# A softmax-minus-one-hot kernel with all large transfers on one queue, in whole blocks and a fixed order

## The chip, the cores and the metric

The kernel runs on one core of a Trainium2 chip. The metric is the device time of one execution in microseconds; lower is better. Bytes move between the chip's main memory and the core's on-chip buffer over sixteen DMA engines, which serve one queue for each engine that issues transfers: here SP's (SyncE's) and ACT's (ScalarE's).

## What is computed

For each of 8 x 1024 rows of 8192 float32 logits the reference computes the softmax and subtracts 1 at the label's place. It is the gradient of a cross entropy.

```python
logits_max = np.max(logits, axis=-1, keepdims=True)
exp_logits = np.exp(logits - logits_max)
softmax = exp_logits / np.sum(exp_logits, axis=-1, keepdims=True)
...
one_hot[batch_idx, seq_idx, labels] = 1.0
return (softmax - one_hot).astype(np.float32)
```

Every logit is read once and every output written once: 268.4 MB in, 268.4 MB out.

## The kernel before

**Tiling.** The 8192 rows are cut into 32 blocks (B) of 256 rows. A block lies as 128 partitions x 2 rows (G = 2) x 8192, so that a partition's two rows are neighbours in memory: 64 KB in one run. A "row" of the code, `t` from 0 to 63, is one of the two 128 x 8192 halves of a block, 4.2 MB; block b holds rows 2b and 2b + 1. The buffer X (line 48) has 3 slots (SLOTS) of one block, and block b uses slot b % 3. All work is done in place.

**One row.** Each operation goes through the helper `run` (lines 70 to 82), which attaches the waits and the semaphore that the operation raises, so most rows of the profile have line 76. `row_max` (line 141) takes the negated maximum on VectorE (TENSOR_REDUCE). `exponentials` takes exp with that bias and the row's sum on ScalarE (ACTIVATE X<-X,m). `mark` makes on ScalarE, in two operations over 2048 words, a byte mask with a 1 at the label (away, then hot, in PSUM, with two places). `finish` takes the reciprocal of the sum on VectorE and then x * r - mask over the row (SCALAR_TENSOR_TENSOR); the last two rows are finished in two halves of 4096 columns each, so that each half can be stored by itself.

**Transfers.** `load` (line 101) and `store` (line 114) issue transfers in pieces that the letters of LOADS and STORES select for each block: "w" is the whole block in one transfer with 64 KB runs, "r" one transfer for each row with 32 KB runs, "s" two transfers for each row, over the even and the odd partitions. Loads are issued on SP's queue, except the odd halves of "s", which go on ACT's. Blocks 0 to 2 are loaded as "s", 3, 4 and 29 to 31 as "r", the rest as "w". Stores are all "r" and are issued on ACT's queue, where each waits for its row's finish; the four half stores of the last block go two on SP and two on ACT. A load waits until the stores of the block that had its slot have landed, and it is issued for block b + 3 after the work of block b.

**Order.** Each engine runs its instructions in the order in which the program issues them. Every letter of ORDER is "r", which interleaves the rows: maximum of t1, finish of t0, exponentials of t1, store of t0, mark; then the next block's first maximum, finish of t1, exponentials of the next row, store of t1, mark, and the load of block b + 3. Before the loop stand the first three loads and the making of the masks' constants. At the end ACT waits for the stores of the last three blocks.

Of the kernel before, what the change touches and what calls it, by code (L numbers as in the profile page):

```python
# [7 lines left out]
P = 128  # L8
G = 2
SLOTS = 3  # L10

LOADS = "sssrrwwwwwwwwwwwwwwwwwwwwwwwwrrr"
STORES = "rrrrrrrrrrrrrrrrrrrrrrrrrrrrrrrr"
ORDER = "rrrrrrrrrrrrrrrrrrrrrrrrrrrrrrrr"


@with_exitstack
def kernel(
# [6 lines left out]
    nc = tc.nc  # L25
# [11 lines left out]
    T = N // P  # L37
    B = T // G
# [3 lines left out]
    o_b = o_nv.rearrange("(b p j) v -> b p j v", p=P, j=G)  # L42
# [4 lines left out]
    X = const.tile([P, SLOTS, G, V], fp32)  # L47
# [11 lines left out]
    m, s, r = (const.tile([P, T], fp32, name=n) for n in ("m", "s", "r"))  # L59
# [4 lines left out]
    with tc.tile_critical():  # L64
        sem = tc.alloc_semaphore
        got = [[sem(f"got{i}{q}") for q in range(4)] for i in range(SLOTS)]
        put = [[sem(f"put{i}{q}") for q in range(4)] for i in range(SLOTS)]
# [3 lines left out]
        def run(engine, waits, counter, method, **operands):  # L71

            waits = list(dict.fromkeys(waits))
            for w in waits[:-1]:
                engine.wait_ge(*w)  # L75
            instruction = getattr(engine, method)(**operands)  # L76
            for w in waits[-1:]:
                instruction._wait_ge(*w)
            step = 16 if method == "dma_start" else 1
            instruction.then_inc(counter, step)  # L80
            count[counter.name] = count.get(counter.name, 0) + step
            return counter, count[counter.name]

        every, rows = slice(0, P), slice(0, G)
        one = [slice(j, j + 1) for j in range(G)]
        halves = [slice(i, P, 2) for i in range(2)]
        sides = [slice(i * V // 2, (i + 1) * V // 2) for i in range(2)]
        PIECES = {
            "r": [(every, js) for js in one],
            "s": [(ps, js) for js in one for ps in halves],  # L90
            "w": [(every, rows)],
        }

# [4 lines left out]
        loaded, stored, sides_done = {}, {}, {}  # L98
        maxed, summed, marked, finished, freed = {}, {}, {}, {}, {}

        def load(b):
            loaded[b] = []
            before = stored.get(b - SLOTS, [])
            for q, piece in enumerate(PIECES[LOADS[b]]):
                ps, js = piece
                free = [w for other, w in before if meets(piece, other)]
                queue = nc.scalar if LOADS[b] == "s" and ps == halves[1] else nc.sync
                w = run(
                    queue, free, got[b % SLOTS][q], "dma_start",
                    out=X[ps, b % SLOTS, js, :], in_=x_b[b, ps, js, :],  # L110
                )
                loaded[b].append((piece, w))

        def store(t):
            b, j = divmod(t, G)
            stored.setdefault(b, [])
            if t >= T - G:
                for i, cs in enumerate(sides):
                    w = run(
                        nc.sync if t == T - G else nc.scalar, [sides_done[t][i]], put[b % SLOTS][G * j + i],  # L120
                        "dma_start", out=o_b[b, every, one[j], cs], in_=X[every, b % SLOTS, one[j], cs],
                    )
                    stored[b].append(((every, one[j]), w))
                return
            for q, piece in enumerate(PIECES[STORES[b]]):
                ps, js = piece
                if js.stop != j + 1:
                    continue
                w = run(
                    nc.scalar, [finished[t]], put[b % SLOTS][q], "dma_start",  # L130
                    out=o_b[b, ps, js, :], in_=X[ps, b % SLOTS, js, :],
                )
                stored[b].append((piece, w))
# [7 lines left out]
        def row_max(t):  # L141
            b, j = divmod(t, G)
            arrived = {w[0].name: w for piece, w in loaded[b] if meets(piece, (every, one[j]))}
            maxed[t] = run(
                nc.vector, arrived.values(), dve, "tensor_reduce",
                out=m[:, t : t + 1], in_=row(t), axis=mybir.AxisListType.X, op=Alu.max, negate=True,
            )

        def exponentials(t):
            w = run(  # L150
                nc.scalar, [maxed[t]], act, "activation",
                out=row(t), in_=row(t), func=Act.Exp, bias=m[:, t : t + 1], scale=1.0,
                accum_out=s[:, t : t + 1],
            )
            summed[t] = w

        def mark(t):
            if t >= T:
                return
            w = run(  # L160
                nc.scalar, ([made] if t < G else [freed[t - G]]) + ([marked[t - 1]] if t else []), act, "activation",
                out=away[:], in_=count16[:], func=Act.Abs, bias=at(word, t), scale=1.0,
            )
            marked[t] = run(
                nc.scalar, [w], act, "activation",
                out=hot[:, t % G, :], in_=away[:], func=Act.Relu, bias=at(unit, t), scale=at(minus, t),
            )

        def finish(t):
            w = run(nc.vector, [summed[t]], dve, "reciprocal", out=r[:, t : t + 1], in_=s[:, t : t + 1])  # L170
            bytes_ = hot[:, t % G, :].bitcast(u8)
            sides_done[t] = []
            for i, c in enumerate(sides if t >= T - G else [slice(0, V)]):
                last = run(
                    nc.vector, [marked[t], w] if i == 0 else [], dve, "scalar_tensor_tensor",
                    out=row(t)[:, c], in0=row(t)[:, c], scalar=r[:, t : t + 1], in1=bytes_[:, c],
                    op0=Alu.mult, op1=Alu.subtract,
                )
                sides_done[t].append(last)
            finished[t] = freed[t] = last  # L180

        w_raw = run(nc.scalar, [], lab_got, "dma_start", out=lab_raw[:], in_=lab_bp)
        for b in range(SLOTS):
            load(b)
        w = run(nc.gpsimd, [], pool, "memset", ap=ident[:], constant=0.0)
        w_ident = run(
            nc.gpsimd, [w], pool, "affine_select",
            out=ident[:], in_=ident[:], compare_op=Alu.not_equal, fill=1.0,
# [8 lines left out]
        for j in range(G):  # L197
            w = run(
                nc.tensor, [w_ident, w_lab], pe, "transpose",
                out=lab_ps[:, j, :], in_=lab_f[:, j, :], identity=ident[:],  # L200
            )
        w = run(nc.vector, [w], dve, "tensor_copy", out=lab[:], in_=lab_ps)
        w = run(
            nc.vector, [w], dve, "tensor_scalar",
            out=part[:], in0=lab[:], scalar1=2, scalar2=None, op0=Alu.arith_shift_right,
        )
        w_word = run(
            nc.vector, [w], dve, "tensor_scalar",
            out=word[:], in0=part[:], scalar1=-1.0, scalar2=None, op0=Alu.mult,
        )  # L210
        w = run(
            nc.vector, [w_word], dve, "tensor_scalar",
            out=lab[:], in0=lab[:], scalar1=3, scalar2=None, op0=Alu.bitwise_and,
        )
        w = run(
            nc.vector, [w], dve, "tensor_copy", out=minus[:], in_=lab[:]
        )
# [3 lines left out]
            out=unit[:], in0=minus[:], scalar1=0.0, scalar2=powers[0], op0=Alu.is_equal, op1=Alu.mult,  # L221
# [15 lines left out]
        nc.scalar.wait_ge(*w_made)  # L237
        made = made_dve

        row_max(0)  # L240
        exponentials(0)
        mark(0)
        mark(1)
        for b in range(B):
            t0, t1 = b * G, b * G + 1
            nxt = t1 + 1
            if ORDER[b] == "b":
                if t0 not in maxed:
                    row_max(t0)
                    exponentials(t0)  # L250
                row_max(t1)
                exponentials(t1)
                finish(t0)
                store(t0)
                mark(t0 + G)
                finish(t1)
                store(t1)
                mark(t1 + G)
                if b + SLOTS < B:
                    load(b + SLOTS)  # L260
                continue
            if t0 not in maxed:
                row_max(t0)
                exponentials(t0)
            row_max(t1)
            finish(t0)
            exponentials(t1)
            store(t0)
            mark(t0 + G)
            ahead = nxt < T and ORDER[b + 1] == "r"  # L270
            if ahead:
                row_max(nxt)
            finish(t1)
            if ahead:
                exponentials(nxt)
            store(t1)
            mark(t1 + G)
            if b + SLOTS < B:
                load(b + SLOTS)
        for b in range(B - SLOTS, B):  # L280
            for _, w in stored[b]:
                nc.scalar.wait_ge(*w)
# [30 lines left out]
```

## Time and profile before

| what | value |
|---|---|
| time, median of 3 runs | 1248.9 us (1247.81 to 1249.44) |
| span of the profiled execution | 1246.6 us (its time with what lies around the span is not shown) |
| TENSOR_REDUCE, 64 of them | 8682 ns each |
| SCALAR_TENSOR_TENSOR over 8192 columns, 62 of them | 8748 ns each |
| read and written | 268.50 MB and 268.44 MB |
| transfers issued on SP / on ACT | 42 / 71 |

How to read the profile: the page gives for each engine its busy time and share of the span. The DMA rows give packets, bytes and how much of the sixteen DMA engines' time each queue's packets took; q1 is SP's queue and q10 is ACT's. A row of groups has the line, engine, operation, output <- inputs, shapes and count, then busy microseconds and mean nanoseconds of one, then the idle time of the engine just before and what ended most of it. A row of windows gives for a stretch its length, the busy time of each engine (and how many instructions ended there), the granted clock of the matrix engine, the mean busy share of the sixteen DMA engines and the rate in GB/s; bytes are counted by packets, so in a window of a few microseconds the rate depends on where its edges fall between packets. A row of DMA issues gives count, KB of one transfer and the median time from issue to landing.

### The profile page before, as it was taken

Reading aid. Unit: us, or ns where it says so; the run is one execution under the profiler, and the core shown is the slowest. Engines: PE = TensorE matmul, PEld = TensorE weight load, DVE = VectorE, ACT = ScalarE, POOL = GpSimd, SP = SyncE. Lnnn points to the kernel's source line nnn. Section 1 sums busy time; section 2 is a strip of 40 time slices with the busy share of each in tenths; the row PEclk is TensorE's granted clock in tenths of the full one; section 3 lists DMA queues with packets and bytes.
Section 4 is the critical chain, followed back from the end, with each engine's and each line's share of the span. In section 5 each row is a group of like instructions: output and inputs, shape, how many; then the busy total and the mean of one; then the engine's idle time right before and its main releaser. Section 6 shows DMA issues by size and latency. Waiting matters only on the chain.

```text
span 1246.6 us, 809 instructions
## 1 busy us (share of the span) xinstructions
PE 0.4 (0%) x2; PEld 0.3 (0%) x2; DVE 1120.2 (90%) x208; ACT 722.7 (58%) x257; POOL 2.3 (0%) x7
## 2 busy tenths in 40 slices
PE   0000000000000000000000000000000000000000
PEld 0000000000000000000000000000000000000000
DVE  5999998889988889888898888998889988899995
ACT  2866664556555565465655655556556555566662
POOL 0000000000000000000000000000000000000000
DMA  9999999999999999999999999999999999999998
GB/s 406 413 431 434 437 432 444 435 437 421 433 429 437 443 423 433 434 431 435 430 441 435 422 435 435 434 440 426 432 434 431 433 446 434 422 430 435 429 434 383
DMA packets 15413, 536.98 MB, mean 431 GB/s; under 512 B 1808, under 2 KB 1808, under 8 KB 1840
## 3 DMA queue, kind: packets, MB, share of 16 engines
q10 hardware_dynamic: 9744, 276.89, 51.5%
q1 hardware_dynamic: 5664, 260.05, 48.3%
q14 instruction: 5, 0.04, 0.0%
HBM read 268.50 MB, written 268.44 MB: 431 GB/s over the span
## 4 chain that ended last, share of the span: by engine, by line
DMA 59%; DVE 26%; issue 11%; ACT 3%; DVEq 0%; ACTq 0%; SPq 0%
DMA X<-in_logits_dram 33%; DMA out_dram<-X 26%; DVE X L76 15%; DVE m L76 10%; ACT X L76 2%; DVEq L64 0%; DVE r L76 0%; ACT hot L76 0%; ACT away L76 0%; ACTq L76 0%; DVEq L75 0%; ACTq L308 0%; SPq L64 0%
## 5 line engine op out<-in xcount | busy, mean ns | idle before, releaser
L76 ACT ACTIVATE X<-X,m 128x8192 f32<-128x8192 f32 x64 | 455.8, 7122 | 365.2 <-DVE m L76 365.2
L76 DVE TENSOR_REDUCE m<-X 128x1 f32<-128x8192 f32 x64 | 555.6, 8682 | 105.4 <-DMA X<-in_logits_dram 105.4
L76 DVE SCALAR_TENSOR_TENSOR X<-X,r,hot 128x8192 f32<-128x8192 f32 (+1 forms) x66 | 560.1, 8489 | 3.8 <-ACT hot L76 1.6
L76 ACT ACTIVATE away<-count,word 128x2048 bf16<-128x2048 int16 x64 | 128.1, 2001 | 127.0 <-DVE X L76 127.0
L76 ACT ACTIVATE hot<-away,unit,minus 128x2048 int32<-128x2048 bf16 x64 | 131.9, 2061 | 2.1
L76 ACT ACTIVATION_READ_ACCUMULATOR X<-X,m 128x1 f32 x64 | 11.9, 186 | 0.0
L76 DVE RECIPROCAL r<-s 128x1 f32<-128x1 f32 x64 | 9.8, 153 | 0.0
L76 ACT ACT_TABLE_LOAD x1 | 1.3, 1283 | 5.3 <-issue 5.3
L76 DVE CAST lab_f<-lab_raw 32x256 f32<-32x256 int32 x1 | 0.5, 536 | 2.7 <-DMA lab_raw<-in_labels_dram 2.7
L76 POOL IOTA count<- 128x2048 int16 x1 | 1.8, 1823 | 0.0
L76 DVE TENSOR_TENSOR unit<-unit,part 128x64 f32<-128x64 f32 x3 | 0.7, 225 | 0.1
L76 DVE CAST lab<-hot 128x64 int32<-128x64 f32 x1 | 0.2, 224 | 0.5 <-PE hot L76 0.5
L76 DVE TENSOR_SCALAR part<-minus 128x64 f32<-128x64 f32 x3 | 0.6, 194 | 0.1
L76 PE MATMUL hot<-ident,lab_f 32*128 32x32 f32 x2 | 0.4, 298 | 3.3 <-DVE lab_f L76 3.3
L76 PEld LDWEIGHTS hot<-ident,lab_f 32*128 32x128 f32 x2 | 0.3, 192 | 3.3 <-DVE lab_f L76 3.3
L76 DVE CAST minus<-lab 128x64 f32<-128x64 int32 x1 | 0.2, 195 | 0.0
L76 DVE TENSOR_SCALAR word<-part 128x64 f32<-128x64 int32 x1 | 0.2, 195 | 0.0
L76 DVE TENSOR_SCALAR lab<-lab 128x64 int32<-128x64 int32 x1 | 0.2, 195 | 0.0
L76 DVE TENSOR_SCALAR unit<-minus 128x64 f32<-128x64 f32 x1 | 0.2, 195 | 0.0
L76 DVE TENSOR_SCALAR part<-lab 128x64 int32<-128x64 int32 x1 | 0.2, 194 | 0.0
L76 DVE TENSOR_SCALAR minus<-unit 128x64 f32<-128x64 f32 x1 | 0.2, 194 | 0.0
L76 POOL TENSOR_SCALAR_AFFINE_SELECT ident<-ident 32x32 f32<-32x32 f32 x1 | 0.2, 203 | 0.1
(5 smaller groups left out, 0.5 us busy)
## 6 DMA issues: line engine op xcount, KB each, us to landing
out_dram<-X ACTq DMA_DIRECT2D x62, 4096.0 KB, 30.4
X<-in_logits_dram SPq DMA_DIRECT2D x10, 4096.0 KB, 28.1
X<-in_logits_dram SPq DMA_DIRECT2D x6, 2048.0 KB, 32.6
X<-in_logits_dram ACTq DMA_DIRECT2D x6, 2048.0 KB, 37.1
out_dram<-X SPq DMA_DIRECT2D x2, 2048.0 KB, 12.7
out_dram<-X ACTq DMA_DIRECT2D x2, 2048.0 KB, 11.9
X<-in_logits_dram SPq DMA_DIRECT2D x24, 33.4
lab_raw<-in_labels_dram ACTq DMA_DIRECT2D x1, 64.0 KB, 1.8
```

What stands on the lines that cost most here:

```text
L76: instruction = getattr(engine, method)(**operands)
```

## The change

- All transfers except the labels' are issued on SP's queue. ACT issues none but the labels'.
- Blocks 0 to 5 and 31 are loaded by rows, 6 to 30 whole. Blocks 0 to 2 and 28 to 30 are stored by rows, 3 to 27 whole; the last block is stored in four half rows, now all on SP. The form "s" is gone.
- `store` is called once for each block, after the work of the block; a whole store waits for the finish of the block's second row.
- The load after the store of block b is that of block b + 3 for b = 0 to 2. After block 3 none is issued (EARLY), so that from block 4 on it is that of block b + 2. After block 27 two are issued (LATE): 29 and 30, and after 28 that of 31.
- The compute order is by block: maximum and exponentials of t0, maximum and exponentials of t1, finish of t0, mark, finish of t1, mark. No operation of the next block stands between them.

```diff
-LOADS = "sssrrwwwwwwwwwwwwwwwwwwwwwwwwrrr"
-STORES = "rrrrrrrrrrrrrrrrrrrrrrrrrrrrrrrr"
-ORDER = "rrrrrrrrrrrrrrrrrrrrrrrrrrrrrrrr"
+EARLY = 3
+LATE = 27
+
+LOADS = "rrrrrrwwwwwwwwwwwwwwwwwwwwwwwwwr"
+STORES = "rrrwwwwwwwwwwwwwwwwwwwwwwwwwrrrr"
...
-                queue = nc.scalar if LOADS[b] == "s" and ps == halves[1] else nc.sync
                 w = run(
-                    queue, free, got[b % SLOTS][q], "dma_start",
+                    nc.sync, free, got[b % SLOTS][q], "dma_start",
...
-        def store(t):
-            b, j = divmod(t, G)
-            stored.setdefault(b, [])
-            if t >= T - G:
...
-                        nc.sync if t == T - G else nc.scalar, [sides_done[t][i]], put[b % SLOTS][G * j + i],
...
+        def store(b):
+            stored[b] = []
+            if b == B - 1:
+                for t in (T - G, T - 1):
...
+                            nc.sync, [sides_done[t][i]], put[b % SLOTS][G * j + i],
...
             for q, piece in enumerate(PIECES[STORES[b]]):
                 ps, js = piece
-                if js.stop != j + 1:
-                    continue
                 w = run(
-                    nc.scalar, [finished[t]], put[b % SLOTS][q], "dma_start",
+                    nc.sync, [finished[b * G + js.stop - 1]], put[b % SLOTS][q], "dma_start",
...
+        def work(b):
+            t0, t1 = b * G, b * G + 1
+            row_max(t0)
+            exponentials(t0)
+            if b == 0:
+                mark(0)
+                mark(1)
+            row_max(t1)
+            exponentials(t1)
+            finish(t0)
+            mark(t0 + G)
+            finish(t1)
+            mark(t1 + G)
+
+        nxt = SLOTS
         for b in range(B):
...
+            work(b)
+            store(b)
+            if b == EARLY:
                 continue
...
+            for _ in range(2 if b == LATE else 1):
+                if nxt < B:
+                    load(nxt)
+                    nxt += 1
```

More of the change, by code (lines that the diff above doesn't have):

```diff
@@ L85 @@
         one = [slice(j, j + 1) for j in range(G)]
-        halves = [slice(i, P, 2) for i in range(2)]
         sides = [slice(i * V // 2, (i + 1) * V // 2) for i in range(2)]
@@ L89 @@
             "r": [(every, js) for js in one],
-            "s": [(ps, js) for js in one for ps in halves],
             "w": [(every, rows)],
@@ L112, in load @@
                 loaded[b].append((piece, w))
-        def store(t):
-            b, j = divmod(t, G)
-            stored.setdefault(b, [])
-            if t >= T - G:
-                for i, cs in enumerate(sides):
-                    w = run(
-                        nc.sync if t == T - G else nc.scalar, [sides_done[t][i]], put[b % SLOTS][G * j + i],
-                        "dma_start", out=o_b[b, every, one[j], cs], in_=X[every, b % SLOTS, one[j], cs],
-                    )
-                    stored[b].append(((every, one[j]), w))
+        def store(b):
+            stored[b] = []
+            if b == B - 1:
+                for t in (T - G, T - 1):
+                    j = t % G
+                    for i, cs in enumerate(sides):
+                        w = run(
+                            nc.sync, [sides_done[t][i]], put[b % SLOTS][G * j + i],
+                            "dma_start", out=o_b[b, every, one[j], cs], in_=X[every, b % SLOTS, one[j], cs],
+                        )
+                        stored[b].append(((every, one[j]), w))
                 return
@@ L238 @@
         made = made_dve
[L240 to L243, printed above, removed]
-        for b in range(B):
[L245 to L260, printed above, removed]
-                continue
[L262 to L279, printed above, removed]
+        def work(b):
[12 more added lines that the diff above has]
+        nxt = SLOTS
+        for b in range(B):
+            work(b)
+            store(b)
+            if b == EARLY:
+                continue
+            for _ in range(2 if b == LATE else 1):
+                if nxt < B:
+                    load(nxt)
+                    nxt += 1
         for b in range(B - SLOTS, B):
```

## The prediction

> **What bounds the kernel now.** I read the page first: busy time, then the DMA rows, then the queues.
>
> ```profile
> span 1246.6 us, 809 instructions
> ...
> PE 0.4 (0%) x2; PEld 0.3 (0%) x2; DVE 1120.2 (90%) x208; ACT 722.7 (58%) x257; POOL 2.3 (0%) x7
> ...
> DMA packets 15413, 536.98 MB, mean 431 GB/s; under 512 B 1808, under 2 KB 1808, under 8 KB 1840
> ## 3 DMA queue, kind: packets, MB, share of 16 engines
> q10 hardware_dynamic: 9744, 276.89, 51.5%
> q1 hardware_dynamic: 5664, 260.05, 48.3%
> ```
>
> VectorE is busy for 90% of the span, but the two transfer queues (q10 is ACT's, q1 is SP's) together fill 51.5 + 48.3 = 99.8% of the sixteen DMA engines. So the transfers are the bound, and VectorE is 10% short of being one. The windows show where the DMA engines move less than their usual rate; the last column is GB/s, the one before it the DMA share.
>
> ```profile
> core 0: us, PE busy (x) PEld busy (x) DVE busy (x) ACT busy (x) POOL busy (x), PEclk, DMA share, GB/s
> 0.00:5.00 5.00, 0.41 (x2) 0.28 (x2) 1.58 (x7) 0.00 (x0) 2.31 (x7) 1.00 0.65 223
> 29.20:58.20 29.00, 0.00 (x0) 0.00 (x0) 27.40 (x6) 26.63 (x11) 0.00 (x0) 1.00 1.01 434
> 58.20:62.80 4.60, 0.00 (x0) 0.00 (x0) 4.60 (x2) 2.52 (x3) 0.00 (x0) 1.00 1.00 342
> 62.80:72.50 9.70, 0.00 (x0) 0.00 (x0) 9.66 (x3) 5.61 (x3) 0.00 (x0) 1.00 1.00 432
> 200.00:1085.00 885.00, 0.00 (x0) 0.00 (x0) 796.30 (x139) 518.52 (x184) 0.00 (x0) 1.00 1.00 433
> 1235.60:1240.40 4.80, 0.00 (x0) 0.00 (x0) 0.00 (x0) 0.00 (x0) 0.00 (x0) 1.00 1.01 430
> 1240.00:1244.00 4.00, 0.00 (x0) 0.00 (x0) 0.00 (x0) 0.00 (x0) 0.00 (x0) 1.00 0.84 360
> 1244.00:1246.60 2.60, 0.00 (x0) 0.00 (x0) 0.00 (x0) 0.00 (x0) 0.00 (x0) 1.00 0.02 6
> ```
>
> All bytes at the steady 433 GB/s are 536.98 MB / 433 = 1240.1 us. What is lost against that rate: 5 x (1 - 223/433) = 2.4 us at the start, 4.6 x (1 - 342/433) = 1.0 us in 58.2 to 62.8, 4 x (1 - 360/433) = 0.7 us and 2.6 us at the end. The sum is 1246.8, the span 1246.6. So nothing is hidden elsewhere: a faster kernel must move the bytes at a better rate or cut the 6.7 us of edges.
>
> **The change, part by part.**
>
> *Fewer, longer packets.* Of the 15413 packets 1808 are the 4-byte notices (16 for each of 113 DMAs). Afterwards 7 blocks load and 6 store as rows (256 packets of 32 KB each), 25 load and 25 store whole (128 packets of 64 KB), and the last block leaves in 512 packets of 16 KB: 1792 + 1536 + 3200 + 3200 + 512 = 10240, where before has 13568 of this data. DMAs fall from 113 to 81, notices by 512. That is 3840 packets fewer. Their price comes from the two queue rows: q10 holds 9744 packets and 276.89 MB in 51.5% of 16 x 1246.6 us, q1 5664 and 260.05 MB in 48.3%. Two equations, "packets x a + MB x c = time", give a = 3.8 ns a packet; the shares are rounded to 0.1%, so a lies between -1.8 and 9.4 ns. The rates of the windows give a second reading: 16 KB runs at 430 and 32 KB runs at 432 GB/s make 5.6 ns. I take 4.7 ns: 3840 x 4.7 / 16 = **1.1 us gained**, bounds -0.4 to 2.3.
>
> *Loads and stores in turn, not mixed.* Today each engine has packets of both queues at hand for most of the span; afterwards one queue holds 8.4 MB of loads, then 8.4 MB of stores. Load-only (434) and store-only (432) stretches ran as fast as the mix (433): I take **0**, with 1 GB/s of 433 either way, 2.9 us, as a bound. Dearer could only be the turn from a load to a store, the second rival below.
>
> *The store's wait on SP.* The store of a block now waits on SP for VectorE's last operation, and behind it in program order stands the load two blocks ahead; behind that load stands VectorE's work on that block. In the steady part the queue reads: load b, store b-1, load b+1, store b. From the end of load b to the place of store b lie 16.78 MB / 433 = 38.75 us of transfers. In that time VectorE must do block b.
>
> ```profile
> L76 DVE TENSOR_REDUCE m<-X 128x1 f32<-128x8192 f32 x64 | 555.6, 8682 | 105.4 <-DMA X<-in_logits_dram 105.4
> L76 DVE SCALAR_TENSOR_TENSOR X<-X,r,hot 128x8192 f32<-128x8192 f32 x62 | 542.4, 8748 | 3.7 <-ACT hot L76 1.6
> L76 ACT ACTIVATE X<-X,m 128x8192 f32<-128x8192 f32 x64 | 455.8, 7122 | 365.2 <-DVE m L76 365.2
> ...
> L76 ACT ACTIVATION_READ_ACCUMULATOR X<-X,m 128x1 f32 x64 | 11.9, 186 | 0.0
> L76 DVE RECIPROCAL r<-s 128x1 f32<-128x1 f32 x64 | 9.8, 153 | 0.0
> ```
>
> Two maxima, two reciprocals, two final operations: 2 x (8.68 + 0.15 + 8.75) = 35.2 us. The new order (both maxima, then both finishes) adds no wait: the first exponentials end at 8.7 + 7.1 + 0.2 = 16.0, before the second maximum ends at 17.4; the second end at 17.4 + 7.3 = 24.7, before the first finish ends at 26.3. So 38.75 - 35.2 = **3.6 us** are left for two latencies: the notice that load b has landed, and the way from SP's issue of the store to its first byte. Before shows neither alone; three rows bound them.
>
> ```profile
> out_dram<-X SPq DMA_DIRECT2D x2, 2048.0 KB, 12.7
> ...
> lab_raw<-in_labels_dram ACTq DMA_DIRECT2D x1, 64.0 KB, 1.8
> ```
>
> The labels' transfer had idle engines: 1.8 us from issue to landing, both latencies and 0.15 us of moving 64 KB. So 1.65 us together. The last stores on SP's queue took 12.7 us for 2.1 MB, which alone are 4.85 us and beside ACT's queue, taking turns, 9.7: both latencies are 3.0 us, or 7.8 if nothing is put down to the other queue. I take 1.8, near the first row, since in one queue nothing stands between. The store then comes 1.8 us early, and the wait costs **0**. Load b+2 behind it waits for store b-1, which landed a load earlier: 0 as well.
>
> *The ends.* Six row loads lie alone on SP's queue, so the first row lands sooner than now.
>
> ```profile
> 15.75 8.69 DVE L76 TENSOR_REDUCE m<-X 128x1 f32<-128x8192 f32 x1 [8.91 <-DMA X<-in_logits_dram]
> ```
>
> It can start near 11 us rather than 15.75, but the queue is then full of loads until 58 us, and VectorE needs the first two rows done only by then (about 51 us with ACT's marks): 0. At the end load 31 stands before stores 29 to 31, 3 x 19.4 us of transfers, while VectorE has at most two blocks of 35.2 us left, of which one is done when the load has landed: 0. The uneven end of the engines (0.7 us) may shrink with one queue: I take 0.3, bounds 0 and 0.7. ACT loses 70 issues and VectorE nothing; neither sets the end.
>
> *Sum.* 1246.6 - 1.1 - 0.3 = 1245.2 us of span. Of the profiled execution only the span is shown; the median of the runs, 1248.9, stands 2.3 us above it, which I take for what lies around a span. With these, **1247.5 us**, 0.11% less. With the bounds: 2.3 + 0.7 us and a little of the 2.9 us of the rate make 1244.6 at the low end, -0.4 and some of the 2.9 make 1249.5 at the high.
>
> **The rivals.**
>
> *1. The same mechanism, more of it.* Packets at the upper bound, an even end, or phases at 434: 1245 to 1246.4, faster by over 0.2%. For it: nothing stands against it but the sizes; the edges that could go are small.
>
> *2. Each turn from load to store in one queue costs (slower).* In 58.2 to 62.8 us ACT's queue ran from its last loads into its first stores, and SP's had just run dry. The engines were busy (share 1.00) and moved 342 GB/s: 1.0 us lost at a turn within one queue. Before has one such turn, as ACT's queue only stores and SP's only loads afterwards. The changed queue has 29: a store behind a load for blocks 0 to 3, 5 to 29 (4, 30 and 31 follow a store). 28 more at 0.97 us are 27 us: 1274.7. It decides from the first turn; nothing covers it, since the DMA engines are the bound. Against it: the mix at 433 GB/s turns at nearly every packet, and the price may be a first filling, or SP's queue running dry.
>
> *3. The store comes late.* If the two latencies exceed 3.6 us, the queue runs dry before the store. The load behind it is put off too, but block b+1 had landed already, so its store gains that time: every second of 25 stores is late, by x - 3.6. At x = 5.4 (between 3.0 and 7.8) 12 x 1.8 = 22 us: 1269. For it: VectorE is the nearest resource to the bound. Against it: two of the three readings stay under 3.6.
>
> The Trainium skill (Perfetto Trace Analysis, DMA Optimizations) advises one engine for inputs and another for outputs, to allow a more dynamic spread. That is what this change gives up, and by that rule the result would be rival 3; here the trace bears it out only in that the two queues never left the engines idle between 200 and 1085 us.
>
> **How the numbers follow.** A measurement of this kernel tells about 0.2% (2.5 us) from no change. No stall: 0.60, of it 0.34 within 0.2% (the forecast) and 0.26 beyond it (rival 1). Rival 2: 0.25. Rival 3: 0.10. Something else, slower: 0.05. So faster 0.26, same 0.34, slower 0.40. The no-stall cases have 1244.6 to 1249.5 as their own range; 0.60 is too little, so the range reaches to the full price of rival 2, 1275, which takes in most of rival 3.
>
> **What the changed profile would show.** Right: one queue with near 99.7% of the sixteen engines, about 11570 packets, 433 to 434 GB/s in the middle, VectorE idle some 3.5 us in each block and always for a load, and SP waiting for VectorE. Rival 2: DMA share still 1.00, but under 428 GB/s. Rival 3: a DMA share under 0.98 with VectorE's idle time unchanged in kind. A span over 1250 us proves the forecast wrong.

## The result and the profile after

The changed kernel takes **1262.7 us** (1261.05 to 1264.52, 4 runs) against 1248.56 for the kernel before in the same sitting. The ratio is 1.0115, with a 95% interval of 1.0100 to 1.0129: 14 us slower. The forecast was 1247.5 and no change; the time lies inside the range, above the cases without a stall (up to 1249.5) and below the prices of rival 3 (1269) and rival 2 (1274.7). One run below, the whole stores on ACT's queue, was profiled in an execution of 1323.9 us where its other three took 1273.3 to 1277.8, so its trace is read for orders of magnitude only.

First the page of the changed kernel: busy time, packets, the queue, and the whole transfers with their median time from issue to landing.

```profile
span 1260.6 us, 747 instructions
...
PE 0.4 (0%) x2; PEld 0.3 (0%) x2; DVE 1120.2 (89%) x208; ACT 722.7 (57%) x257; POOL 2.3 (0%) x7
...
DMA packets 11574, 536.99 MB, mean 426 GB/s; under 512 B 1296, under 2 KB 1296, under 8 KB 1328
...
q1 hardware_dynamic: 11520, 536.88, 99.5%
...
out_dram<-X SPq DMA_DIRECT2D x25, 23.7
X<-in_logits_dram SPq DMA_DIRECT2D x25, 43.1
```

The change does what it says: one queue, 11574 packets (11570 were counted ahead). VectorE has the same work. The DMA engines are marked busy for 99.5%, and yet they move 426 instead of 431 GB/s. The windows of the changed kernel show where; the last two columns are the DMA share and GB/s.

```profile
29.20:58.20 29.00, 0.00 (x0) 0.00 (x0) 24.97 (x6) 23.30 (x12) 0.00 (x0) 1.00 1.01 434
58.20:62.80 4.60, 0.00 (x0) 0.00 (x0) 4.60 (x2) 0.60 (x1) 0.00 (x0) 1.00 0.94 342
200.00:400.00 200.00, 0.00 (x0) 0.00 (x0) 172.97 (x31) 112.78 (x40) 0.00 (x0) 1.00 1.01 434
400.00:600.00 200.00, 0.00 (x0) 0.00 (x0) 178.26 (x32) 113.05 (x41) 0.00 (x0) 1.00 0.99 425
600.00:800.00 200.00, 0.00 (x0) 0.00 (x0) 177.96 (x31) 116.14 (x41) 0.00 (x0) 1.00 1.01 430
800.00:1000.00 200.00, 0.00 (x0) 0.00 (x0) 177.38 (x31) 115.57 (x41) 0.00 (x0) 1.00 1.00 425
200.00:1085.00 885.00, 0.00 (x0) 0.00 (x0) 782.80 (x136) 507.71 (x179) 0.00 (x0) 1.00 1.00 428
1250.00:1260.60 10.60, 0.00 (x0) 0.00 (x0) 0.00 (x0) 0.00 (x0) 0.00 (x0) 1.00 0.59 250
```

The middle lost 885 x (1 - 428/433) = 10.2 us, and the loss begins late: the first 200 us of it run at 434. The last window is compared with the same length at the end of the kernel before:

```profile
1236.00:1246.60 10.60, 0.00 (x0) 0.00 (x0) 0.00 (x0) 0.00 (x0) 0.00 (x0) 1.00 0.69 297
```

There it ran at 297 GB/s, here at 250: 10.6 x (297 - 250)/433 = 1.2 us more. Another 1.5 us went between 1085 and 1250 us, at 428 GB/s where the kernel before had 432 from 1085 to 1236. The three make 12.9 of the 14.0 us between the spans. The first turn from loads to stores costs what it did before, 342 GB/s in the same window.

Why the middle begins well is in the timeline, first at 228, then at 587 us. A row has start, length, engine and operation; in brackets the idle time before.

```profile
228.08 0.33 SPq L77 DMA_DIRECT2D out_dram<-X  x1
228.45 0.43 SPq L77 DMA_DIRECT2D X<-in_logits_dram  x1
238.16 17.28 DVE L77 TENSOR_REDUCE m<-X 128x1 f32<-128x8192 f32 x2 [10.11 <-DMA X<-in_logits_dram]
...
552.27 17.28 DVE L77 TENSOR_REDUCE m<-X 128x1 f32<-128x8192 f32 x2 [5.15 <-DMA X<-in_logits_dram]
...
578.51 8.75 DVE L77 SCALAR_TENSOR_TENSOR X<-X,r,hot 128x8192 f32<-128x8192 f32 x1
587.29 0.33 SPq L77 DMA_DIRECT2D out_dram<-X  x1
587.66 0.43 SPq L77 DMA_DIRECT2D X<-in_logits_dram  x1
591.00 17.28 DVE L77 TENSOR_REDUCE m<-X 128x1 f32<-128x8192 f32 x2 [3.74 <-DMA X<-in_logits_dram]
```

VectorE starts on a block when the last of the sixteen DMA engines has given notice. From 552.27 to 587.29 it needs 35.0 us, as forecast. At 228 us the store is issued ten microseconds before the load ahead of it has landed (238.16). At 587 it is issued 3.7 us before (591.00). That still looks early. But the trace's notices of that load came from 587.87 (first engine) to 590.98 (last): the engines are 3.1 us apart. For the first ones the store was issued 0.6 us before their notice. The packet records show it: on fourteen engines the last packet of the load ended from 587.57 us on, and their first packet of the store started at 588.12, 0.8 us after the issue. They had run dry. The other two engines were one packet behind and ran on without a gap.

The same notices, read for the slowest engine, give each transfer's time as the step from one landing to the next. The 25 whole stores took 19.37 us on average, the 25 whole loads 19.94. Where a store was issued over 1.6 us ahead of the first notice of the load before it, the load behind that store took 19.60 us (mean of 9); where it was issued later, 20.10 (mean of 14); a load with nothing in its way takes 19.3. So the price of a late store shows at the load behind it: 25 x (19.94 - 19.33) = 15 us. The two groups overlap (19.3 to 20.3 and 19.4 to 20.8); these times follow the slowest engine alone.

The packet records of all sixteen engines give a clearer picture. A 64 KB packet mostly takes 2.42 us; around the end of the store that landed at 610 us some took up to 3.5. What the packets around the end of a whole store took beyond 2.42 us, per engine, was 0.88 us on average where the store had been issued under 1 us ahead of that first notice (3 stores), 0.65 at 1 to 1.5 us (9), 0.22 at 1.5 to 2 (6) and 0.06 at over 2 (5). Between 200 and 1085 us such longer packets make 11.4 us per engine, against 3.1 with the half maximum, the first experiment below; the time without any packet differs by only 1.7 us between the two. So for the most part the engines did not stand idle for a late store: they were slow at the turn behind it.

### The profile page after: what moved, and what is told of

It reads as the page before. It is cut to its first block, busy times and chain, and to the rows that moved or that the text cites. A ratio compares the mean times of both kernels' runs of the same rounds, so it can differ in the third digit from the quotient of the medians.

```text
span 1260.6 us, 747 instructions
## 1 busy us (share of the span) xinstructions
PE 0.4 (0%) x2; PEld 0.3 (0%) x2; DVE 1120.2 (89%) x208; ACT 722.7 (57%) x257; POOL 2.3 (0%) x7
## 2 busy tenths in 40 slices
DMA packets 11574, 536.99 MB, mean 426 GB/s; under 512 B 1296, under 2 KB 1296, under 8 KB 1328
## 3 DMA queue, kind: packets, MB, share of 16 engines
q1 hardware_dynamic: 11520, 536.88, 99.5%
## 4 chain that ended last, share of the span: by engine, by line
DVE 50%; DMA 43%; issue 4%; ACT 2%; SPq 0%
DMA X<-in_logits_dram 43%; DVE X L77 25%; DVE m L77 25%; ACT X L77 1%; DVE r L77 1%; ACT hot L77 0%; SPq L77 0%; ACT away L77 0%; SPq L289 0%; SPq L65 0%
## 6 DMA issues: line engine op xcount, KB each, us to landing
X<-in_logits_dram SPq DMA_DIRECT2D x14, 4096.0 KB, 19.4
out_dram<-X SPq DMA_DIRECT2D x25, 23.7
```

## The experiments

Theory A: the store comes late. Theory B: each turn between loads and stores within one queue costs. All are compared with the kernel before, which took 1248.2 to 1248.6 us in each sitting. Differences are to the changed kernel's 1262.7, which was not measured again in the later sittings. The half maximum, the stores by rows, the rows in turn and the whole stores on ACT's queue ran on one chip, the other experiments on another.

### A shorter chain on VectorE

```diff
-                out=m[:, t : t + 1], in_=row(t), axis=mybir.AxisListType.X, op=Alu.max, negate=True,
+                out=m[:, t : t + 1], in_=row(t)[:, : V // 2], axis=mybir.AxisListType.X, op=Alu.max, negate=True,
```

> The changed kernel, but each row's maximum is taken over its first 4096 columns only (the bias of the exponentials; the rest of the row is left out of the maximum). Every transfer, its size, queue and order stay; VectorE's work for a block falls by 2 x 4.3 = 8.7 us, so each whole store is issued some 8.7 us earlier. Theory A (the store comes late: load, 35 us of VectorE and the issue fill the 38.6 us that the queue gives them): the 14 us go, 1246 to 1249 us. Theory B (each turn from load to store or back within one queue costs some 0.5 us whenever the store is issued): stays at 1262.

Measured: 1250.8 us, ratio 1.0019 (1.0010 to 1.0028). 12 of the 14 us go with no transfer changed, so theory A holds and B, which has the same turns, falls. The windows of this run, the middle and the last 10.6 us:

```profile
200.00:1085.00 885.00, 0.00 (x0) 0.00 (x0) 584.16 (x133) 493.80 (x176) 0.00 (x0) 1.00 1.00 433
1240.70:1251.30 10.60, 0.00 (x0) 0.00 (x0) 0.00 (x0) 0.00 (x0) 0.00 (x0) 1.00 0.43 182
```

The middle is back at 433. The end is worse than ever, 182 GB/s: 10.6 x (297 - 182)/433 = 2.8 us more than before, since some engines finish long after others: the notices of the last store lie 6.5 us apart.

### Stores by rows, and rows in turn

```diff
-STORES = "rrrwwwwwwwwwwwwwwwwwwwwwwwwwrrrr"
+STORES = "rrrrrrrrrrrrrrrrrrrrrrrrrrrrrrrr"
```

> The changed kernel with all stores by rows (32 KB runs), still on SP in the same order: the first row's store is issued some 8.8 us before the second's, which is wanted 9.7 us later. Nothing is left out. Theory A: the late store is gone, and 3200 packets more cost about 1 us: 1247 to 1250 us. Theory B: as many turns as before, 1262 to 1264.

Measured: 1253.5 us, ratio 1.0037 (1.0024 to 1.0049). 9 us go; 3.5 more than the upper end of theory A's expectation stay. The load behind the stores was issued no earlier than in the changed kernel: from 300 us on 16.5 to 20.4 us ahead of the first notice of the store it follows, there 20.6 to 21.6. So what counts is when the store was issued, not when the load behind it was. The next kernel also loads by rows and, between block 4 and 26, alternates them:

```diff
+            if EARLY < b < LATE:
+                for j in range(G):
+                    store(b, j)
+                    load(nxt, j)
+                nxt += 1
+                continue
```

> The changed kernel with all transfers by rows, and from block 4 to 26 the one queue holds store of row 0, load of row 0, store of row 1, load of row 1: twice as many turns, and each store is wanted later than it is issued by over 8 us. Nothing is left out. Theory A: 1247 to 1250 us (some 1 to 2 us of it for the shorter packets). Theory B: the price of the turns doubles, near 1276.

Measured: 1251.7 us, ratio 1.0025 (1.0016 to 1.0035). Twice as many turns and 11 us faster: a turn whose store was issued in time costs nothing that can be seen. The middle and the end of both, rows by stores first:

```profile
200.00:1085.00 885.00, 0.00 (x0) 0.00 (x0) 788.42 (x138) 511.63 (x181) 0.00 (x0) 1.00 1.00 432
1242.10:1252.70 10.60, 0.00 (x0) 0.00 (x0) 0.00 (x0) 0.00 (x0) 0.00 (x0) 1.00 0.56 238
```

```profile
200.00:1085.00 885.00, 0.00 (x0) 0.00 (x0) 798.97 (x139) 517.40 (x184) 0.00 (x0) 1.00 1.00 432
1240.20:1250.80 10.60, 0.00 (x0) 0.00 (x0) 0.00 (x0) 0.00 (x0) 0.00 (x0) 1.00 0.48 204
```

Again the middle is mended and the end is not.

### Whole stores on ACT's queue

```diff
-                    nc.sync, [finished[b * G + js.stop - 1]], put[b % SLOTS][q], "dma_start",
+                    nc.scalar, [finished[b * G + js.stop - 1]], put[b % SLOTS][q], "dma_start",
```

> The changed kernel with the whole stores and the row stores (all but the last block's) issued on ACT's queue instead of SP's; sizes, lead and compute order stay. Theory A: a late store no longer leaves the DMA engines dry, since the next load does not stand behind it: 1246 to 1250 us. Theory B: no turns within one queue, so 1246 to 1250 as well. If it stays near 1262, neither the queue nor its order is the cause, but the whole stores or the compute order.

Measured: 1276.9 us, ratio 1.0218 (1.0201 to 1.0236): both theories missed, it is 14 us slower still. The whole transfers in its trace (span 1322.1 us), from issue to landing:

```profile
out_dram<-X ACTq DMA_DIRECT2D x25, 44.0
X<-in_logits_dram SPq DMA_DIRECT2D x25, 41.3
```

In this trace each whole store, beside a load, takes 44.0 us, where the one queue needs 23.7. A load two blocks ahead waits for that landing to get its slot. That this wait is what costs the 14 us is argued, not shown; the next run bears it out only in part, as it makes the stores smaller.

### Row stores on ACT's queue

The edit to row stores and the edit to ACT's queue, together.

> The changed kernel with all stores by rows and on ACT's queue (the last block's four half rows stay on SP): loads, their lead of two and the order of work by block stay. If whole stores beside loads on two queues are what made the run with ACT's stores 15 us slower still (each 8.4 MB transfer then takes 44 us, and the load behind waits for its landing), rows give it back: 1249 to 1254 us. If the order of work by block is what costs, it stays above 1265.

Measured: 1249.2 us, ratio 1.0010 (1.0000 to 1.0019). Against the row stores on SP (1253.5) the kernel differs in the queue alone: two queues are some 4 us better here, measured on two chips. The order of work by block, with the other changes to the loads, leaves 1 us against before. Middle and end of this run:

```profile
200.00:1085.00 885.00, 0.00 (x0) 0.00 (x0) 796.12 (x138) 517.94 (x184) 0.00 (x0) 1.00 1.00 433
1237.00:1247.60 10.60, 0.00 (x0) 0.00 (x0) 0.00 (x0) 0.00 (x0) 0.00 (x0) 1.00 0.66 281
```

### How much earlier is early enough

The maximum over 7/8, 15/16 and 3/4 of the row (`row(t)[:, : 7 * V // 8]` and so on), and one maximum more:

```diff
+            run(
+                nc.vector, arrived.values(), dve, "tensor_reduce",
+                out=r[:, t : t + 1], in_=row(t)[:, : V // 8], axis=mybir.AxisListType.X, op=Alu.max, negate=True,
+            )
```

> The changed kernel with each row's maximum over 7/8 of its columns (the last eighth is left out of the maximum): VectorE's chain for a block is 2.2 us shorter, all else stays. Theory A (the store comes late by little: 0.8 to 1.1 us from issue to first byte where 1.8 cost nothing in the trace of the changed kernel): most of the loss goes, 1250 to 1253 us. Theory C (VectorE's load as such, in proportion): a quarter of what the half maximum took away, 1259 to 1260.

> The same with the maximum over 15/16 of the columns (the last sixteenth is left out): the chain is 1.1 us shorter. Theory A: about half of the loss or more goes, 1252 to 1258 us. Theory C: an eighth, 1261.

> The changed kernel with one more maximum over an eighth of each row, whose result goes where the reciprocal is written later: the chain is 2 x 1.1 = 2.2 us longer, the result the same. VectorE's work on a block becomes 37.4 us, still under the 38.6 us of transfers. Theory A: the round of a store, the load behind it and VectorE's work on that load holds two blocks' transfers and one chain, so each two blocks take 2.2 us more: 12 x 2.2 = 26 us, 1285 to 1292. Theory B (turns): the time stays, 1262 to 1264.

> The changed kernel with the maximum over 3/4 of each row (the last quarter is left out of it): the chain is 4.4 us shorter, between the 7/8 (1258.2) and the half (1250.8). Theory A in the form that the two shorter steps leave (the DMA engines drift apart until the first of them run dry again, so the price fades with the slack and does not stop at once): 1253 to 1256 us.

| chain against the changed kernel | time, us | middle, GB/s | first to last notice at 800 to 900 us | last 10.6 us, GB/s |
|---|---|---|---|---|
| + 2.2 us | 1271.0 | 424 | 0.5 us | 346 |
| as changed | 1262.7 | 428 | 2.7 | 250 |
| - 1.1 us | 1259.5 | 430 | 3.5 | 252 |
| - 2.2 us | 1258.2 | 430 | 4.5 | 235 |
| - 4.4 us | 1255.5 | 431 | 5.3 | 221 |
| - 8.7 us | 1250.8 | 433 | 6.4 | 182 |

Theory A as I first put it missed three of these: 2.2 us were not enough to end the loss (1258.2, not 1250 to 1253), 1.1 us gave 3.2 rather than half of 14 or more, and the longer chain cost 8.3 us and not 26. Theory C, in proportion, would have 1259 to 1260, and 1261 for 1.1 us. That is 1 to 2 us too slow both times, but within the 95% intervals (about 1.9 us either way), so these steps do not exclude it; the longer chain, some 5 us above proportion, and the next experiment, in which VectorE has all of its work and the loss is gone, do. The fourth, made from what the others showed, came within its bounds (1255.5 in 1253 to 1256). The fourth column tells why there is no edge: with more slack the DMA engines drift further apart, until the stores come less than 2 us ahead of the leading ones again. That this drift uses the slack up is read from the table; it was not tried by itself.

Most of the longer chain's price stands in one place. First windows of that run:

```profile
200.00:400.00 200.00, 0.00 (x0) 0.00 (x0) 189.19 (x41) 112.78 (x40) 0.00 (x0) 1.00 0.99 419
400.00:600.00 200.00, 0.00 (x0) 0.00 (x0) 186.48 (x41) 114.78 (x41) 0.00 (x0) 1.00 0.99 425
```

The first 200 us run at 419 (the changed kernel: 434), 200 x (1 - 419/434) = 6.9 us, where all engines ran dry before the store of block 4; afterwards it runs at 425 as the changed kernel does. My 26 us counted two blocks' transfers in a round; a round from landing to landing holds one store and one load, 38.7 us, the chain of 37.2 and about 1.2 of latencies: 77.1, still within the 77.3 that the queue needs for two blocks.

### Whole stores, issued early, with nothing left out

```diff
-LOADS = "rrrrrrwwwwwwwwwwwwwwwwwwwwwwwwwr"
+LOADS = "rrrrrrrrrrrrrrrrrrrrrrrrrrrrrrrr"
```

> The changed kernel with all loads by rows and the stores as they are, whole from block 3 to 27. VectorE can take the first row's maximum while the second row is still arriving, so a block's store is issued some 8.7 us earlier, with nothing left out. Theory A (late whole stores): 1250 to 1253 us, as with the half maximum, 3200 packets more included. If whole stores on one queue cost for another reason than their time of issue (their 64 KB runs, say), it stays near 1262.

Measured: 1250.5 us, ratio 1.0016 (1.0006 to 1.0025). With the first row's maximum taken while the second row arrives, the whole stores cost nothing in the middle any more: 12 us come back from changing the loads. VectorE does the same work as in the changed kernel, so neither that work as such (theory C) nor the size of the stores by itself is the cause. The middle and end:

```profile
200.00:1085.00 885.00, 0.00 (x0) 0.00 (x0) 800.74 (x139) 518.77 (x184) 0.00 (x0) 1.00 1.00 433
1237.70:1248.30 10.60, 0.00 (x0) 0.00 (x0) 0.00 (x0) 0.00 (x0) 0.00 (x0) 1.00 0.59 250
```

No version beat the kernel before.

## Why the prediction was wrong

- **The bound** was right: the transfers, and nothing but a rate or an edge could change the time. Both changed, the wrong way.
- **Packets**: the count was right (3840 fewer). The 1.1 us was not measured alone; 434 GB/s in the part without late stores does not speak against it.
- **Loads and stores in turn, price 0**: right where the store was issued in time. 434 GB/s from 200 to 400 us, and twice as many turns cost nothing. The 1.0 us of the first turn comes once, and rival 2, which made 27 us of it, is refuted.
- **The store's wait: this is the step that failed.** "So 38.75 - 35.2 = 3.6 us are left for two latencies" left out a third term. The chain was right (35.0), the latencies even shorter than taken: 0.3 us from an engine's last packet to its notice and 0.8 from issue to first packet, against 1.8. The Trainium skill (DMA: Bandwidth & Descriptors, Specifications) gives about 0.6 us to the first byte for these queues; the trace has 0.8. But the sum was made as if the sixteen engines were one. VectorE starts after the last engine's notice, and the store must be in the queue before the first engine is done: the 3.1 us between them belong into the sum, 3.6 - 1.1 - 3.1 = -0.6. The trace of the kernel before had such a distance too, 2.9 us on average between the first and the last notice of a transfer at 800 to 900 us. And it is not enough to come just before an engine runs dry: only stores issued some 2 us ahead of the first notice left the packets at their usual length, and 3.6 - 3.1 leaves 0.5. The wait that was put at 0 goes with a loss of 10.2 us between 200 and 1085 us, which an earlier store takes away.
- **Rival 3** had the place (a late store), the rhythm (about every second store) and the sign; its price, 1269, came from an assumed latency. It had 0.10. Its sign in the profile was put wrongly too: a DMA share under 0.98 was to show it, and the share stayed at 1.00 while the rate fell, as the packets' own records grew longer. The profile looked much like the sign of rival 2 (share 1.00, 428 GB/s), and only the runs told the two apart.
- **The range** holds the measured time, and that is luck: it reached beyond 1249.5 for the price of rival 2, which is refuted.
- **The rule of the Trainium skill** (Perfetto Trace Analysis, DMA Optimizations), one issuing engine for inputs and another for outputs: the pair with row stores agrees (1249.2 against 1253.5 us); with whole stores it is the other way (1276.9 against 1262.7).
- **The ends**: that the uneven end of the engines "may shrink with one queue" was wrong. It grew, by 1.2 us in the changed kernel and by up to 2.8 in the experiments that mended the middle. At the start VectorE's first maximum began at 13.40 us, not near 11, and as forecast that cost nothing: the first 72.5 us run at 413 GB/s in both kernels.

So the 14 us come apart in this way: 9.2 us for whole stores instead of rows (1262.7 to 1253.5), 4.3 for SP's queue instead of ACT's under the row stores (to 1249.2), about 1 for the rest. That split holds in this order of steps only, since the queue's effect changes its sign with the size of the stores, and the later steps were measured on another chip.

What stays open: why a store that is issued under 2 us ahead makes packets longer at its own end, some 20 us later, and why engines that had their store in good time also lost there, wasn't settled. Why the engines drift apart was not settled either.

## What to carry to other kernels

Where one in-order queue carries loads and stores, count the slack of a store from the last engine's notice to the first engine's last packet, not from the end of one transfer to the start of the next. Here VectorE's 35.0 of 38.75 us left too little room for that. If the large store is wanted, make the compute start on a part of the load, which gave 12 us here. A second queue for stores paid here with stores of one row, and not with stores of a whole block.

## What the runs showed of the hardware

- The sixteen DMA engines do not keep in step on one queue: the notices of one transfer lay 0.3 to 0.8 us apart in the first 100 us, and after 1000 us 6.8 us apart on average with the half maximum and 6.3 with the row stores on SP. With the longer chain, where stores came late from the start, they stayed within 1.5 us.
- On this queue an engine's first packet came 0.8 us after the issue, and the notice 0.3 us after its last packet (at 587 us in the changed kernel).
- Packets around the end of a store get longer when it was issued late: 0.88 us per engine for stores under 1 us ahead of the first notice of the transfer before them, 0.06 for those over 2 us ahead.
- Two 8.4 MB transfers on two queues at once took 44.0 us (store) and 41.3 us (load) to land in the one trace there is of it (span 1322.1 us).
- A DMA share of 1.00 does not mean full speed: 425 and 434 GB/s were both seen at shares of 0.99 to 1.01.
